# A third Strassen product of the second block's MLP output map made from seven quarter products

## The chip, the cores and the metric

The kernel runs on one core of one Trainium2 chip. The metric is the device time of one execution in microseconds (us); less is better. TensorE (PE in the profile) multiplies, VectorE (DVE) and ScalarE (ACT) work element by element, GpSimd (POOL) and SyncE (SP) mostly issue transfers.

## The reference

One decoder layer on 2048 tokens of width 1024: a token-mixing sub-layer (an input projection, a gated short convolution, a causal pooling, an output projection) and an MLP of hidden width 4096, each closed by a residual sum and a LayerNorm.

```
h = x * (1.0 + sc1) + sh1
z = h @ w_in[l]
...
x = _layer_norm(DEEPNORM_ALPHA * x + (1.0 + g1) * mix, ln1_g[l], ln1_b[l])
h = x * (1.0 + sc2) + sh2
f = jnp.square(jax.nn.relu(h @ w_mlp_in[l])) @ w_mlp_out[l]
x = _layer_norm(DEEPNORM_ALPHA * x + (1.0 + g2) * f, ln2_g[l], ln2_b[l])
```

The change sits in the second matrix of the MLP, `w_mlp_out` (4096 by 1024).

## The kernel before

**Blocks.** The tokens are worked in two blocks of 1024 (b = 0 and 1), one after the other: input projection (in_proj_1 for block 1), output projection with the first LayerNorm, `up()` (the first MLP map with the squared ReLU) and `down()` (the second map, with the second LayerNorm in the class Close).

**Precision.** Each fp32 operand is split into a high part (a ScalarE cast, L81) and a low part (a VectorE subtraction, L82), and a product is three matmuls, high by high, high by low, low by high (L86 to L88, in `mm3`). The low part waits for the cast, and the matmuls wait for both. `tt` (L91) is the helper for all other VectorE sums.

**Seven products for eight.** The large products are cut into 2 by 2 blocks and made by Strassen's scheme in Winograd's form, seven products instead of eight:

```
ORDER = (("11", "11"), ("12", "21"), ("s2", "2"), ("s1", "1"), ("s3", "3"), ("s4", "22"), ("22", "4"))
```

Each entry names the left block or sum (U, the activations; s1 to s4 are sums of blocks) and the right one (W; 1 to 4 are sums). `up()` makes the U blocks and their sums and stores them in DRAM (`usum`, or `uquart` for those needed in quarters); `down()` loads them with the weights, splits them and multiplies.

**down() of block 1.** Products are taken in steps: a coarse product i has two halves (hf) of four operand pairs, and each half is 96 matmuls of 128x512 into four PSUM banks X[0..3] or Y[0..3], one for each of four tiles of 128 tokens. In most steps the loop is over operands, then tiles; in the second halves of products 3, 4 and 6 ("by tile") it is over tiles, then operands, so that each tile's result can be finished while the next is made. Products 1 and 5 are "fine": each is again made as seven products of quarter blocks, each of 48 matmuls of 128x256 (L1118), with sums in SBUF tiles F[0..7]. Before, the order is product 0 (two steps), the 14 fine products, then 2, 3, 4 and 6. The finished rows are handled by `third_row` and `first_row` (tiles 0 to 3, behind product 3), `second_row` (behind 4) and `last` and `last_part` (tiles 4 to 7, behind 6, the tail of the kernel; tile 7 is cut into two column quarters). They add the banks, multiply by the gate (`gate`, g2), add the saved residual (`rsave`) and normalise.

**residual()** loads the normalised input `nsave[t]` of each token tile, scales and shifts it by two VectorE operations, and stores it in `rsave[t]`; `down()` lets it go on by two tiles a step from step n = 2.

**Sums for quarters.** A fine product needs sums of quarter blocks: of U, made by `save_quarters` in `up()`, and of W, made by `sum_blocks` behind `up()`'s later groups g (QUARTER_SUMS says how many behind each) and stored in `wquart`.

**Order.** The queue of each engine is fixed when the program is built: the framework schedules the instructions in a list, and each engine works strictly along its own. So an instruction that waits holds up everything behind it on its engine. Buffers rotate through pools (t_r, t_w, t_h, t_o and t_ps for PSUM banks).

## Time and profile before

| | us |
|---|---|
| Median of three runs | 1734.39 (1733.82 to 1734.42) |
| Profiled execution, its own time | 1734.73 |
| Its span in the trace | 1733.0 |
| TensorE busy in the span | 1720.9 (99%) |
| VectorE busy | 1342.6 (77%) |
| ScalarE busy | 879.5 (51%) |

The times are those of one execution of the whole program; the span runs from its first to its last instruction. A row of a timeline reads: start, duration, engine, line, operation, tile written and tiles read with shapes, and in brackets the idle time ahead of it with what ended it. Matmuls are pipelined, so their durations overlap, and the distance between starts is what one costs; the same holds, by some 0.08 us, for VectorE. In a list of waits a row gives the total, how many and the longest. The granted clock was 0.999 of full speed.

### The profile page before, as it was taken

To read this page: it belongs to the slowest core of one execution; us is meant where nothing else is said; L and a number is where in the kernel's file an instruction comes from. 1 tells how busy PE (TensorE), PEld (TensorE's weight loads), DVE (VectorE), ACT (ScalarE), POOL (GpSimd) and SP (SyncE) were. 2 spreads that over 40 slices of the span, in tenths; PEclk is the share of its full clock that TensorE was granted. 3 is DMA by queue.
4 is the path that set the end of the run, shared out by engine and by line. 5 is a ranking of instruction groups with operands and counts; after the bars stand their busy time and mean duration, and the time that the engine had idled before them with its cause. 6 is when DMAs were issued, how large, how long until landed. Compare 5 with 4: busy or idle time off the path is not lost.

```text
span 1733.0 us, 22349 instructions
## 1 busy us (share of the span) xinstructions
PE 1720.9 (99%) x7998; PEld 1439.4 (83%) x7998; DVE 1342.6 (77%) x1759; ACT 879.5 (51%) x1188; POOL 235.7 (14%) x441
## 2 busy tenths in 40 slices
PE   9999999999999999999999999999999999999997
PEld 8888888888888888888888888888888888998886
DVE  8898798877777676769686779687677768987894
ACT  5323358554454654436573344775444565763451
POOL 0222221122322000000000000103222221000000
PEclk9999999999999999999999999999999999999999
DMA  9899867778888998887572265657655599998871
GB/s 385 343 322 357 321 229 282 280 272 318 327 320 325 366 413 326 303 289 270 190 273 79 104 236 201 218 196 263 248 205 213 201 325 409 417 362 311 285 257 49
DMA packets 149646, 480.47 MB, mean 277 GB/s; under 512 B 17680, under 2 KB 18464, under 8 KB 149536
## 3 DMA queue, kind: packets, MB, share of 16 engines
q1 hardware_dynamic: 102528, 313.87, 49.8%
q0 software_dynamic: 47008, 165.19, 25.0%
q8 instruction: 62, 1.02, 0.2%
q14 instruction: 48, 0.39, 0.1%
HBM read 329.56 MB, written 149.43 MB: 276 GB/s over the span
## 4 chain that ended last, share of the span: by engine, by line
PE 95%; DVE 2%; issue 2%; DMA 1%; ACT 0%; POOL 0%; SPq 0%; DVEq 0%; POOLq 0%; ACTq 0%
PE ps L86 29%; PE ps L87 29%; PE ps L88 29%; PE ps L1118 5%; PE ps L406 3%; PE ps L757 1%; DVE o L91 1%; DMA r<-msum 1%; DMA msum<-o 0%; DMA r<-in_opening 0%; DVE o L1333 0%; DVE o L1339 0%; DVE o L261 0%; DVE st L726 0%; DVE h L82 0%
## 5 line engine op out<-in xcount | busy, mean ns | idle before, releaser
L87 PE MATMUL ps<-h,w 128*128 128x512 f32 x1312 | 510.3, 389 | 0.0
L88 PE MATMUL ps<-h,w 128*128 128x512 f32 x1312 | 510.1, 389 | 0.0
L86 PE MATMUL ps<-h,w 128*128 128x512 f32 x1312 | 510.1, 389 | 0.0
L86 PE MATMUL ps<-h,h 128*128 128x512 f32 (+1 forms) x1000 | 387.9, 388 | 2.2 <-DVE o L91 1.7
L88 PE MATMUL ps<-h,h 128*128 128x512 f32 (+1 forms) x1000 | 387.7, 388 | 0.0
L87 PE MATMUL ps<-h,h 128*128 128x512 f32 (+1 forms) x1000 | 387.5, 387 | 0.0
L81 ACT CAST h<-r 128x1024 fp32r<-128x1024 f32 (+1 forms) x196 | 199.4, 1021 | 279.0 <-PE ps L87 147.5
L82 DVE TENSOR_TENSOR h<-r,h 128x1024 fp32r<-128x1024 f32 (+1 forms) x196 | 230.9, 1182 | 83.4 <-ACT h L81 83.1
L81 ACT CAST w<-r 128x1024 fp32r<-128x1024 f32 x156 | 164.2, 1053 | 257.0 <-PE ps L87 251.2
L87 PEld LDWEIGHTS ps<-h,w 128*128 128x128 f32 x1312 | 246.3, 188 | 51.8 <-DVE h L82 0.5
L88 PEld LDWEIGHTS ps<-h,w 128*128 128x128 f32 x1312 | 246.3, 188 | 51.1
L86 PEld LDWEIGHTS ps<-h,w 128*128 128x128 f32 x1312 | 246.0, 188 | 51.4 <-issue 0.3
L82 DVE TENSOR_TENSOR w<-r,w 128x1024 fp32r<-128x1024 f32 x156 | 190.6, 1222 | 96.5 <-ACT w L81 95.5
L86 PEld LDWEIGHTS ps<-h,h 128*128 128x128 f32 x1000 | 187.8, 188 | 41.3 <-DVE o L91 1.9
L88 PEld LDWEIGHTS ps<-h,h 128*128 128x128 f32 x1000 | 187.8, 188 | 38.5
L87 PEld LDWEIGHTS ps<-h,h 128*128 128x128 f32 x1000 | 187.8, 188 | 38.0
L91 DVE TENSOR_TENSOR o<-o,o 128x1024 f32<-128x1024 f32 (+2 forms) x218 | 186.0, 859 | 42.8 <-DMA usum<-o 39.2
L82 DVE TENSOR_TENSOR h<-w,h 128x1024 fp32r<-128x1024 f32 x124 | 151.2, 1219 | 4.9 <-ACT h L81 4.8
L91 DVE TENSOR_TENSOR o<-o,ps 128x512 f32<-128x512 f32 (+1 forms) x172 | 112.4, 664 | 48.6 <-PE ps L88 48.2
L81 ACT CAST h<-w 128x1024 fp32r<-128x1024 f32 x124 | 130.0, 1049 | 9.5 <-DMA w<-in_w 4.3
L1003 POOL DMA_DIRECT2D usum<-o x96 | 51.7, 538 | 431.9 <-ACT o L997 195.8
L91 DVE TENSOR_TENSOR r<-r,r 128x1024 f32<-128x1024 f32 x60 | 73.4, 1223 | 11.4 <-DMA r<-in_w 7.6
(151 smaller groups left out, 1419.3 us busy)
## 6 DMA issues: line engine op xcount, KB each, us to landing
usum<-o POOLq DMA_DIRECT2D x96, 512.0 KB, 4.2
r<-usum SPq DMA_DIRECT2D x96, 512.0 KB, 5.3
w<-w2sum SPq DMA_DIRECT2D x64, 512.0 KB, 6.1
r<-in_w SPq DMA_DIRECT2D x60, 512.0 KB, 5.8
o<-in_w SPq DMA_DIRECT2D x72, 256.0 KB, 5.8
w2sum<-o POOLq DMA_DIRECT2D x64, 256.0 KB, 6.0
w<-in_w SPq DMA_DIRECT2D x32, 512.0 KB, 6.0
r<-uquart SPq DMA_DIRECT2D x28, 512.0 KB, 9.5
```

The lines of the kernel that those rows point to most:

```text
L81: high = nc.scalar.copy(hi, src)
L82: return high.ins, nc.vector.tensor_tensor(lo, src, hi.bitcast(F32), op=ALU.subtract).ins
L86: nc.tensor.matmul(ps, whi, xhi, start=first, stop=False, skip_group_check=goes_on)
L87: nc.tensor.matmul(ps, whi, xlo, start=False, stop=False, skip_group_check=goes_on)
L88: nc.tensor.matmul(ps, wlo, xhi, start=False, stop=last, skip_group_check=goes_on)
L91: return nc.vector.tensor_tensor(out_, a, b_, op=op)
L406: nc.tensor.matmul(ps[m, h], wt[:, w : w + P], A[k][p // 2][:, hs], start=k == 0 and p == 0, stop=k == KD - 1 and p == 2)
L757: nc.tensor.transpose(ps[:, t * P : t * P + P], R[4 * h + t][:, k * P : k * P + P], ident)
L1003: nc.gpsimd.dma_start(usum[g, i], r)
L1118: nc.tensor.matmul(ps, a[:, us], w[:, gs], start=not begun, stop=hf == 1 and g == 3 and a is ul, skip_group_check=True)
```

## The change

Product 0 of block 1's map (11 by 11) becomes fine too: `FINE` gets an entry for it, and `coarse` drops it, so 192 matmuls of 128x512 give way to 336 of 128x256. The order is now product 2 (coarse), 21 fine products (0, 1, 5), then 3, 4, 6.

- The quarters of product 0 are summed in F[4..7]. ScalarE copies them once to the other half; after product 1 and after product 5 four VectorE adds join them to F[0..3], and after product 5 product 2's banks X are added as well. `third_row` now adds (it copied), and `last` adds the bank to F before the gate, where the gate read the bank.
- The sums of W quarters and some of U quarters are generators in two `Spare` lists. `sums_beside.step()` puts the next VectorE operation of such a sum behind a product: 14 steps in groups 1 and 2 of `in_proj_1`, the rest in `up()` from g = 1. The weights for it come as whole 128x1024 tiles (`w2s`). For g = 0 and 1 the block of U for product 0 is stored whole and loaded again for its quarter sums.
- `residual()` begins at step 0 and gives its eight tiles in five turns, ending at 0, 1, 4, 6 and 7.
- For tile 7 the first halves are added ahead of the last step, and its last two quarters go to two PSUM banks of their own (`ps = t_ps()`), where both used X[3].
- In `in_proj_1`'s last group `pool_mid` stands behind the first half of the convolution.

The core of the diff (line numbers of helpers move by one, L82 becomes L81, L91 becomes L90):

```diff
+    class Spare:
+        def __init__(self):
+            self.items = []
+            self.current = None
+
+        def add(self, item):
+            self.items.append(item)
+
+        def step(self, n=1):
+            for _ in range(n):
+                while True:
+                    if self.current is None:
+                        if not self.items:
+                            return
+                        self.current = self.items.pop(0)
+                    if next(self.current, self) is not self:
+                        break
+                    self.current = None
...
+    sums_beside, quarters_beside = Spare(), Spare()
+
+    def quarter_sums(n, hf, p):
+        a, b_ = t_o(T), t_o(T)
+        b22, b12, b11, b21 = a[:, :H], a[:, H:], b_[:, :H], b_[:, H:]
+        for i, r in enumerate((a, b_)):
+            nc.sync.dma_start(r, w2s[n, hf, p, i])
+        yield
+        tt(b22, b22, b12, ALU.subtract)
+        yield
+        tt(b12, b12, b11, ALU.subtract)
+        yield
+        tt(b11, b22, b11, ALU.add)
+        yield
+        tt(b21, b21, b11, ALU.subtract)
+        for i, r in ((2, b22), (0, b12), (1, b11), (3, b21)):
+            nc.gpsimd.dma_start(wquart[n, hf, i][:, p * H : p * H + H], r)
+
+    for n_ in (2, 0, 1):
+        for hf_ in range(2):
+            for p_ in range(2):
+                sums_beside.add(quarter_sums(n_, hf_, p_))
...
+        def beside_(j):
+            if 0 < j < NG - 1:
+                sums_beside.step()
...
-                pt = pool_mid(1, j, v)
...
+                    pt = pool_mid(1, j, v)
...
-    FINE = {1: 0, 5: 1}
+    FINE = {0: 2, 1: 0, 5: 1}
+    QUARTERED = {1: 0, 7: 1, 0: 2}
...
-            if fine and i in (1, 7):
-                save_quarters(r, i // 4, g)
-            else:
-                nc.gpsimd.dma_start(usum[g, i], r)
+            if fine and i in QUARTERED and (i or g > 1):
+                item = save_quarters(r, QUARTERED[i], g)
+                quarters_beside.add(item)
+                if i == 0:
+                    kept.append(item)
+                return
+            nc.gpsimd.dma_start(usum[g, i], r)
+            if fine and i == 0:
+                sums_beside.items.insert(0, save_quarters(None, QUARTERED[i], g, True))
...
+        def beside_():
+            if fine and g:
+                quarters_beside.step(2)
+                if g > 1:
+                    sums_beside.step()
...
-            if t % 2:
+            if t in ends:
...
-        coarse = (0, 2, 3, 4, 6) if b else (0, 1, 2, 3, 5, 4, 6)
+        coarse = (2, 3, 4, 6) if b else (0, 1, 2, 3, 5, 4, 6)
...
-            return [F[2 * row + t][:, c : c + Q] for t in range(2)]
+            return [F[(0 if i else 4) + 2 * row + t][:, c : c + Q] for t in range(2)]
...
+                ps = t_ps()
                 for n, (uh, ul, wh, wl) in enumerate(ops):
                     for p in range(2):
                         cs = slice(p * H + 3 * P, p * H + 4 * P)
                         ws_ = slice(p * H + c, p * H + c + Q)
-                        mm3(banks[3][:, c : c + Q], uh[:, cs], ul[:, cs], wh[:, ws_], wl[:, ws_],
-                            False, n == len(ops) - 1 and p == 1, True)
-                last_part(slice(c, c + Q), banks[3][:, c : c + Q])
+                        mm3(ps[:, :Q], uh[:, cs], ul[:, cs], wh[:, ws_], wl[:, ws_],
+                            n == p == 0, n == len(ops) - 1 and p == 1)
+                last_part(slice(c, c + Q), ps[:, :Q])
...
-            keep(t + 4, hi_, ps)
+            add(t + 4, hi_, ps)
...
+            if b:
+                tt(F[t + 4][:, lo_], F[t + 4][:, lo_], ps, ALU.add)
+                ps = F[t + 4][:, lo_]
...
-            table[0] = X, True, lambda t, ps: None
-            table[2] = X, False, lambda t, ps: add(t, hi_, ps)
+            table[2] = X, True, lambda t, ps: None
             table[3] = Y, True, third_row
-        base = 2 if b else 5
+        base, turns = (0, 5) if b else (5, 4)
...
-        later = residual()
+        later = residual((0, 1, 4, 6, 7) if b else (1, 3, 5, 7))
...
+                if b and i == 6:
+                    add(7, lo_, X[3])
+                    gate(7, lo_)
+                    tt(rest[6][3], rest[6][3], F[7][:, lo_], ALU.add)
...
-                    if m == 6:
-                        for t in range(4):
-                            add(t, lo_, X[t])
+                    if part_ < 6:
+                        continue
+                    for t in range(4):
+                        if k == 0:
+                            nc.scalar.copy(F[t + 4][:, hi_], F[t + 4][:, lo_])
+                            continue
+                        cs = lo_ if k == 1 else hi_
+                        tt(F[t][:, cs], F[t][:, cs], F[t + 4][:, lo_], ALU.add)
+                        if k == 5:
+                            add(t, hi_, X[t])
...
-        else:
-            sums = [(sum_blocks, [w2q[n, i, hf] for i in range(4)], wquart[n, hf], p)
-                    for n in range(2) for hf in range(2) for p in halves]
```

The change shows in the queues at these three places, the first two on VectorE and TensorE, the third on VectorE.

VectorE in `in_proj_1` of block 1, where group 3's product 2 begins. `w` low parts come from L82 (now L81); the `ps` rows add product 1's two banks, L261 and L265 (now L260 and L264) are steps of the pooling and the convolution. Before:

```order
L326 SCALAR_TENSOR_TENSOR o_7867<-o_7792,vecs,o_7867 128x1024
L643 COPY o_8046<-uhalo 128x2
L82 TENSOR_TENSOR w_8150<-r_8047,w_8149 128x1024
L327 SCALAR_TENSOR_TENSOR o_7867<-o_7792,vecs,o_7867 128x1024
L91 TENSOR_TENSOR o_7867<-o_7867,o_7868 128x1024
L261 TENSOR_TENSOR o_8121<-o_7791 128x1039
L82 TENSOR_TENSOR w_8180<-r_8144,w_8179 128x1024
L91 TENSOR_TENSOR o_8045<-o_8045,ps_8093 128x512
L261 TENSOR_TENSOR o_8123<-o_8121 128x1037
L91 TENSOR_TENSOR o_8046<-o_8046,ps_8106 128x512
```

Now:

```order
L326 SCALAR_TENSOR_TENSOR o_7895<-o_7810,vecs,o_7895 128x1024
L90 TENSOR_TENSOR r_8089<-r_8089,r_8088 128x1024
L260 TENSOR_TENSOR o_8162<-o_7809 128x1039
L90 TENSOR_TENSOR o_7895<-o_7895,o_7896 128x1024
L260 TENSOR_TENSOR o_8164<-o_8162 128x1037
L90 TENSOR_TENSOR o_8086<-o_8086,ps_8134 128x512
L260 TENSOR_TENSOR o_8166<-o_8164 128x1033
L90 TENSOR_TENSOR o_8087<-o_8087,ps_8147 128x512
L264 SCALAR_TENSOR_TENSOR o_8168<-o_8166,o_7809 128x1024
L81 TENSOR_TENSOR w_8191<-r_8088,w_8190 128x1024
```

The split that gives product 2's first low weights (w_8150 before, w_8191 now) stood ahead of both bank adds and stands behind them and behind the L264 step.

TensorE at the same place. The bank ps_8100 is product 2's first; w_8190 is the high and w_8191 the low part of its weights. Now:

```order
L87 MATMUL ps_8147<-h_7065,w_8131 128x512
L85 MATMUL ps_8100<-h_7074,w_8190 128x512
L86 MATMUL ps_8100<-h_7075,w_8190 128x512
L85 MATMUL ps_8113<-h_7074,w_8190 128x512
L86 MATMUL ps_8113<-h_7075,w_8190 128x512
L85 MATMUL ps_8224<-h_7288,w_8220 128x512
L87 MATMUL ps_8100<-h_7074,w_8191 128x512
L85 MATMUL ps_8100<-h_7074,w_8190 128x512
L86 MATMUL ps_8100<-h_7075,w_8190 128x512
```

Five matmuls come between product 1's last and the first that reads w_8191; before, the third matmul of the product read w_8150.

VectorE in `down()` of block 1, from `third_row`'s first tile (bank ps_13212 before, ps_13542 now). Before:

```order
L91 TENSOR_TENSOR o_11442<-o_11442,ps_13212 128x512
L91 TENSOR_TENSOR o_11442<-o_11442,bc_4830 128x1024
L1323 SCALAR_TENSOR_TENSOR o_11442,mv_13399<-o_11442,r_13396 128x512 x2
L734 TENSOR_SCALAR mv_13399<-mv_13399 128x1
L1333 SCALAR_TENSOR_TENSOR o_13406<-o_11442,mv_13399,w_13402 128x1024
```

Now:

```order
L90 TENSOR_TENSOR o_11540<-o_11540,ps_13542 128x512
L90 TENSOR_TENSOR o_11536<-o_11536,ps_13542 128x512
L90 TENSOR_TENSOR o_11536<-o_11536,bc_4830 128x1024
L90 TENSOR_TENSOR r_13690<-r_13690,o_11640 128x1024
L90 TENSOR_TENSOR r_13695<-r_13695,o_11640 128x1024
L90 TENSOR_TENSOR r_13690<-r_13690,o_11642 128x1024
L90 TENSOR_TENSOR r_13695<-r_13695,o_11642 128x1024
L1429 SCALAR_TENSOR_TENSOR o_11536,mv_13729<-o_11536,r_13726 128x512 x2
L90 TENSOR_TENSOR o_11541<-o_11541,ps_13543 128x512
```

One more add and four operations of the residual (r_13690 and r_13695 are tiles 5 and 6) have come between; the residual's were ahead of `third_row` before.

VectorE at the end of that list, the last splits for product 4's second half. Before:

```order
L719 TENSOR_SCALAR mv_13545<-mv_13545 128x1
L82 TENSOR_TENSOR h_13597<-w_13590,h_13596 128x1024
L718 RECIPROCAL mv_13545<-mv_13545 128x1
L82 TENSOR_TENSOR h_13605<-r_13600,h_13604 128x1024
L82 TENSOR_TENSOR h_13609<-w_13602,h_13608 128x1024
```

Now:

```order
L81 TENSOR_TENSOR h_13915<-w_13908,h_13914 128x1024
L775 RECIPROCAL mv_13875<-mv_13875 128x1
L81 TENSOR_TENSOR h_13923<-r_13918,h_13922 128x1024
L81 TENSOR_TENSOR h_13927<-w_13920,h_13926 128x1024
L81 TENSOR_TENSOR h_13935<-r_13930,h_13934 128x1024
L90 TENSOR_TENSOR r_13942<-r_13942,o_11640 128x1024
L81 TENSOR_TENSOR h_13939<-w_13932,h_13938 128x1024
```

An operation of the residual's tile 7 (r_13942) stands ahead of the last split.

TensorE there; h_13934 and h_13938 are the last operand pair's high parts, h_13935 and h_13939 its low ones, ps_11651 and ps_11652 the banks of the first and second tile. Now:

```order
L87 MATMUL ps_11651<-h_13926,h_13923 128x512
L85 MATMUL ps_11651<-h_13938,h_13934 128x512
L85 MATMUL ps_11652<-h_13902,h_13898 128x512
L86 MATMUL ps_11652<-h_13903,h_13898 128x512
L87 MATMUL ps_11652<-h_13902,h_13899 128x512
L85 MATMUL ps_11652<-h_13902,h_13898 128x512
L86 MATMUL ps_11651<-h_13939,h_13934 128x512
L87 MATMUL ps_11651<-h_13938,h_13935 128x512
```

Four matmuls of the second tile stand ahead of the first that reads h_13939; before, the tile's matmuls stood in one row without them.

VectorE in the tail, tile 4 of eight and the start of tile 5 (L783 is L726 before, L1439 is L1333, L1445 is L1339). Before:

```order
L91 TENSOR_TENSOR o_11446<-ps_11546,bc_4830 128x512
L91 TENSOR_TENSOR o_11446<-o_11446,r_14020 128x512
L726 BN_STATS st_13789<-o_11446 128x6
L730 BN_AGGR mv_14052<-st_13789 128x2
L719 TENSOR_SCALAR mv_14052<-mv_14052 128x1
L718 RECIPROCAL mv_14052<-mv_14052 128x1
L1333 SCALAR_TENSOR_TENSOR o_14050<-o_11446,mv_14052,w_13402 128x1024
L1339 SCALAR_TENSOR_TENSOR o_14050<-o_14050,mv_14052,w_13404 128x1024
L91 TENSOR_TENSOR o_11447<-ps_11547,bc_4830 128x512
```

Now:

```order
L90 TENSOR_TENSOR o_11540<-o_11540,ps_11651 128x512
L90 TENSOR_TENSOR o_11540<-o_11540,bc_4830 128x512
L90 TENSOR_TENSOR o_11540<-o_11540,r_14355 128x512
L783 BN_STATS st_14124<-o_11540 128x6
L787 BN_AGGR mv_14391<-st_14124 128x2
L776 TENSOR_SCALAR mv_14391<-mv_14391 128x1
L775 RECIPROCAL mv_14391<-mv_14391 128x1
L1439 SCALAR_TENSOR_TENSOR o_14389<-o_11540,mv_14391,w_13732 128x1024
L1445 SCALAR_TENSOR_TENSOR o_14389<-o_14389,mv_14391,w_13734 128x1024
L90 TENSOR_TENSOR o_11541<-o_11541,ps_11652 128x512
```

Each tile has one more L90 row, the add of the bank.

More of the change, by code (lines that the diff above doesn't have):

```diff
@@ L44, in tile_hybrid_layer @@
 def tile_hybrid_layer(ctx: ExitStack, tc: tile.TileContext, opening, xT, x, wada, vec, win0, win,
-                      wins, wpool, wout, wmix, w1, w2, w2q, rows, out):
+                      wins, wpool, wout, wmix, w1, w2, w2q, w2s, rows, out):
     nc = tc.nc
@@ L1009, in up @@
         save(c11, 0)
+        beside_()
         yield
@@ L1033, in up @@
             join(c12, Z)
+            beside_()
+        for item in kept:
+            quarters_beside.finish(item)
         s1 = t_o()
@@ L1047, in up @@
         save(c11, 7)
+        beside_()
+        if fine and g == NC - 1:
+            quarters_beside.step(99)
+            sums_beside.step(99)
     def down_operands(i, gs):
@@ L1064, in down_operands, with residual @@
         return out_, done
-    def residual():
+    def residual(ends):
         ag, ab = row(t_o(D), rows[0]), row(t_o(D), rows[1])
@@ L1146, in down, with matmuls @@
         fine_banks = {}
-        def matmuls(banks, ops, new, begins, ends, then, by_tile, cut=False):
+        def matmuls(banks, ops, new, begins, ends, then, by_tile, cut=False, closes=False):
             if new and begins:
@@ L1162, in matmuls @@
                     mm3(banks[t], uh[:, cs], ul[:, cs], wh[:, ws_], wl[:, ws_],
-                        new and begins and n == p == 0, ends and n == len(ops) - 1 and p == 1, not new)
+                        new and begins and n == p == 0,
+                        (ends or closes and t == 3) and n == len(ops) - 1 and p == 1, not new)
                 if ends and n == len(ops) - 1:
@@ L1394, in mlp @@
                 pass
-            some = (QUARTER_SUMS if b else HALF_SUMS)[g]
+            some = HALF_SUMS[g]
             for make, src, dst, p in sums[:some]:
```

45 lines of the change are left out of this document (36 added, 9 removed).

## The prediction

> **What bounds it now.** I read the page first, then its chain of work, then TensorE's list of waits.
>
> ```profile
> PE 1720.9 (99%) x7998; PEld 1439.4 (83%) x7998; DVE 1342.6 (77%) x1759; ACT 879.5 (51%) x1188; POOL 235.7 (14%) x441
> PE 95%; DVE 2%; issue 2%; DMA 1%; ACT 0%; POOL 0%; SPq 0%; DVEq 0%; POOLq 0%; ACTq 0%
> PE ps L86 <- DVE o L91: 1.7, 1, 1.7
> PE ps L120 <- DVE tmp L115: 1.1, 1, 1.1
> PE ps L406 <- ACT h L222: 0.6, 1, 0.6
> PE ps L86 <- ACT o L628: 0.6, 1, 0.6
> ```
>
> TensorE is busy for 99% of the span and is 95% of the chain; in the whole run it waits four times, 4.0 us together. So the time moves in only two ways: TensorE gets less or more to stream, or a wait comes or goes. The waits must be looked for where VectorE or ScalarE prepares operands with little time to spare, because VectorE gets most of the added work. An average of 77% says nothing about those places.
>
> **The product itself.** Chain and timeline give the first matmul of the coarse product 0, the first fine one, and the whole fine stage; then ScalarE's two longest waits in that stage (total, times, longest), and a window of it (columns: PE, PEld, DVE, ACT, POOL busy, clock, DMA share, GB/s).
>
> ```profile
> 1424.18 0.39 PE L86 MATMUL ps<-h,h 128*128 128x512 f32 x1
> 1467.70 0.76 PE L1118 MATMUL ps<-h,h 128*128 128x256 f32 x5
> 1467.87 80.63 PE ps L1118 x672
> 1548.50 0.23 PE ps L86
> ACT h L81 <- PE ps L1118: 15.6, 22, 0.9
> ACT h L81 <- DMA r<-uquart: 0.6, 3, 0.3
> 1468.00:1488.00 20.00, 20.00 (x169) 20.00 (x169) 18.45 (x18) 16.23 (x20) 0.00 (x0) 1.00 1.03 418
> ```
>
> The coarse product takes 1467.70 − 1424.18 = 43.52 us for 192 matmuls, 0.2267 each. The fine stage takes 80.63 us for 672, 0.1200 each. Seven quarter products are 7 × 48 = 336 matmuls, 40.32 us. Term 1 is 40.32 − 43.52 = **−3.2 us**. This holds as long as TensorE stays the bound of the longer fine stage. ScalarE waits there for TensorE to free operand buffers, not the other way, VectorE has 1.55 us of 20 free, and the adds between the groups (four of 0.6) fall into operands prepared a product ahead. The DMA share of 1.03 is full, with the transfers still ahead of the casts; I cost it at nothing and keep it as a rival.
>
> [...] The rows (226.7 and 120.0) show a fixed part of 2 × 120.0 − 226.7 = 13.3 ns for these fp32r triples, so halving the columns pays less, and I keep −3.2.
>
> **The sums moved into the mixing projection (in_proj_1).** Fourteen steps of the quarter sums now stand behind products of its groups 1 and 2. Going through the order, I find one place where a split that TensorE is about to need moves behind them: the switch to group 3's product 2.
>
> ```profile
> 992.00:1014.00 22.00, 22.00 (x98) 18.20 (x97) 21.93 (x23) 10.06 (x14) 0.71 (x1) 1.00 0.32 112
> 1000.36 1.22 DVE L82 TENSOR_TENSOR w<-r,w 128x1024 fp32r<-128x1024 f32 x1
> 1006.24 0.68 DVE L91 TENSOR_TENSOR o<-o,ps 128x512 f32<-128x512 f32 x1
> 1006.84 1.23 DVE L261 TENSOR_TENSOR o<-o 128x1037 f32<-128x1037 f32 x1
> 1007.99 0.68 DVE L91 TENSOR_TENSOR o<-o,ps 128x512 f32<-128x512 f32 x1
> 1010.87 1.22 DVE L265 SCALAR_TENSOR_TENSOR o<-o,o 128x1024 f32<-128x1024 f32 x1
> 1007.44 0.39 PE L88 MATMUL ps<-h,w 128*128 128x512 f32 x1
> 1007.67 0.39 PE L86 MATMUL ps<-h,w 128*128 128x512 f32 x1
> ```
>
> VectorE works 21.93 of 22 us here. The split that gives this product's low weights ran at 1000.36, 7.3 us ahead of its first matmul at 1007.67. In the changed order it stands behind the add of product 1's second bank, which cannot begin before that bank is done (the row at 1007.99), and behind the last step of the convolution. So 1007.99 + 0.60 (add; rows 1006.24 and 1006.84 stand 0.60 apart) + 1.2 (L265) + 1.14 (split) = 1010.9. The matmul order fills in five others first, so the low part is needed at 1007.67 + 5 × 0.2267 = 1008.8. Term 2 is **+2.1 us**. Bounds: 0, if scheduling makes an operand look later than it is, and 4, if the extra work ahead (two weight sums and the wait-free adds) makes the queue another 2 us late. I take 2.1, as these rows give it directly.
>
> The later end of this projection had one wait:
>
> ```profile
> 1044.62 0.48 ACT o L628
> 1045.14 0.50 PE ps L86
> ```
>
> The last mixed sums are placed three to four VectorE operations earlier relative to their neighbours, and TensorE arrives 2 us later, so the copy at L628 should no longer be late: term 3, **−0.6 us** (0 if it stays).
>
> **The sums moved into up().** Two VectorE operations behind each product, some 12 us in all.
>
> ```profile
> 1130.00:1423.00 293.00, 293.00 (x1295) 242.32 (x1294) 215.84 (x257) 154.89 (x182) 61.64 (x103) 1.00 0.63 231
> ```
>
> VectorE has 77 us idle in 293, and the DMA share is 0.63. The cover is that idle time; without it the 12 us would stand on the path at most once. The closing quarter sums of before disappear here, and residual tiles take their place. The transfers count too: an item loads two 512 KB tiles on SyncE's queue and stores four slices on GpSimd's (22 and 24 more instructions there in the whole order), at a DMA share of 0.63. The four copies that ScalarE makes once after the first seven products are of 0.5 us each (its L628 copy, above), in a stage where it works 16.23 of 20. I cost all this at **0** (−1 to +2).
>
> **The end of the map: product 4, second half.** This is the place to watch. Coarse steps are 21.76 us. The rows give the starts of product 3's second half (1613.64) and product 4's second half (1657.16), and VectorE between them.
>
> ```profile
> 1616.00:1638.00 22.00, 22.00 (x99) 18.22 (x98) 21.17 (x32) 8.61 (x18) 1.07 (x2) 1.00 0.76 266
> 1638.00:1661.00 23.00, 23.00 (x103) 19.04 (x102) 23.00 (x37) 19.19 (x34) 0.00 (x0) 1.00 0.88 299
> 1612.76 1.23 DVE L91 TENSOR_TENSOR r<-r,o 128x1024 f32<-128x1024 f32 x1 [6.58 <-DMA r<-nsave]
> 1616.18 3.62 DVE L91 TENSOR_TENSOR r<-r,o 128x1024 f32<-128x1024 f32 x3
> 1621.98 0.68 DVE L91 TENSOR_TENSOR o<-o,ps 128x512 f32<-128x512 f32 x1
> 1655.73 1.21 DVE L82 TENSOR_TENSOR h<-w,h 128x1024 fp32r<-128x1024 f32 x1
> 1656.87 1.21 DVE L82 TENSOR_TENSOR h<-r,h 128x1024 fp32r<-128x1024 f32 x1
> 1613.64 0.39 PE L86 MATMUL ps<-h,h 128*128 128x512 f32 x1
> 1657.16 0.39 PE L86 MATMUL ps<-h,h 128*128 128x512 f32 x1
> ```
>
> From the first add of third_row (1621.98) to the end of the last split that product 4's second half needs (1656.87) VectorE is solidly busy: 34.9 us. This step goes tile by tile, so all four operands are needed within its first tile. The same list in the changed order holds four more bank adds (0.60 each, 2.4) and five more residual operations (3.53 / 3 = 1.18 to 1.14 each, 5.7): 34.9 + 8.1 = 43.0 us. When may it begin? Not before the first tile of product 3 is done, 5.6 us after that step's start, and in before it began 8.3 after it (1621.98 − 1613.64), held up by residual loads (the 6.58). So it ends 48.6 to 51.3 after the start. The new matmul order fills in four matmuls of the second tile, so the last low part is needed 43.52 + 23 × 0.2267 = 48.7 after it. The wait is 0 to 2.6, and more if one of the queue's own waits (a residual load, a square root on ScalarE) grows: up to 5. Term 4 is **+2 us**, near the row 1621.98, because the same loads and more splits stand ahead of the list.
>
> **The tail.** Tiles 4 to 6 of the last product get one more bank add each; the last two quarters go to banks of their own.
>
> ```profile
> 1706.32 0.69 DVE L91 TENSOR_TENSOR o<-ps,bc 128x512 f32<-128x512 f32 x1 [15.97 <-PE ps L88]
> 1707.05 0.69 DVE L91 TENSOR_TENSOR o<-o,r 128x512 f32<-128x512 f32 x1
> 1711.76 0.69 DVE L91 TENSOR_TENSOR o<-ps,bc 128x512 f32<-128x512 f32 x1
> 1721.22 0.42 DVE L91 TENSOR_TENSOR o<-ps,bc 128x256 f32<-128x256 f32 x1
> 1721.69 0.39 PE L86 MATMUL ps<-h,h 128*128 128x256 f32 x1 [1.66 <-DVE o L91]
> 1724.87 0.42 DVE L91 TENSOR_TENSOR o<-ps,bc 128x256 f32<-128x256 f32 x1 [1.24 <-PE ps L88]
> 1726.24 0.26 DVE L730 BATCH_NORM_AGGREGATE mv<-st 128x2 f32<-128x24 f32 x1
> ```
>
> VectorE needs 5.44 us a tile (1711.76 − 1706.32), the same as 24 matmuls, so it only just keeps up. One more add of 0.73 (1707.05 − 1706.32) in each of three tiles makes VectorE the bound: the tiles start at 1706.32, 1712.49 and 1718.66. The 1.66 us that TensorE waited for VectorE's read of the shared bank disappear, and the second quarter's sums would be ready by 1724.87 − 1.66 = 1723.2; but VectorE, 2.2 us late, aggregates the last tile's statistics at 1727.2 instead of 1726.24. Term 5 is **+0.95 us** (0.5 to 1.5), and the vanished wait is worth nothing.
>
> **Sum.** −3.2 + 2.1 − 0.6 + 0 + 2.0 + 0.95 = +1.25 against the profiled run's own 1734.73 (span 1733.0): 1736.0. The median of the runs shown is 1734.39, 0.34 lower, so 1735.6. A measurement here can tell about 0.2%, 3.5 us, from no change.
>
> **Rivals.** (a) Both new waits are absorbed, because the splits are ready: −3.2 − 0.6 + 0.95 = −2.85, 1731.5. For it: the margins are 2 us out of long queues. Against it: VectorE shows no idle time in either place. (b) The other side: the list before product 4's second half begins 8.3 us or later and one of its ten small waits on ScalarE, or a residual load behind the full DMA queues (share 0.88), costs 2 to 3 us more. It decides from a wait of 4.5 us there. With 5 us, and the other terms as summed, +4.3: 1738.7; with 4 at term 2 as well, 1740.6. (c) The longer fine stage is bound by its transfers: a share of 1.03 over 121 us instead of 81. For it: ScalarE waits for `uquart` three times, 0.6 us in all; against it: TensorE never did in 80 us. If 40 us of it ran 5% late, +2: 1737.6. (d) The product's gain is kept whole, with the terms at their low ends (0, −0.6, −1, 0, +0.5): −4.3, 1730.1, faster.
>
> **Numbers.** The forecast gets 0.40 (1733.5 to 1737.8), (a) 0.24, (b) 0.20, (c) 0.06, (d) 0.10. Slower by over 0.2% (above 1737.9) takes (b), half of (c) and the forecast's upper edge: 0.29. Faster (below 1730.9) takes (d) and a little of (a): 0.13. The rest, 0.58, is within. For 8 times in 10 the range reaches from 1731.0 into (a) to 1741.0, the end of (b).
>
> **What would show it.** Fine stage: 1008 matmuls in 121 us without a wait. In the list of TensorE's waits, one on a weight's split (L81) of about 2 us near 1009 and one on an operand's split near the middle of the last coarse steps; neither the wait for L628's successor nor the 1.7 on the shared bank. VectorE's tail tiles 6.17 us apart. I'm wrong if the splits are ready in time at both places, or if TensorE waits in the fine stage or in up().

## The result, and the profile after

The changed kernel takes 1747.41 us (median of 4 runs, 1743.96 to 1748.01) against 1734.2 for the one before: ratio 1.0072, 95% interval 1.0055 to 1.0090. It is slower by about 13 us, outside the forecast's range. The profiled execution took 1748.01 us with a span of 1746.2.

Busy times, chain of work and TensorE's waits of the changed kernel:

```profile
PE 1722.0 (99%) x8142; PEld 1444.0 (83%) x8142; DVE 1382.4 (79%) x1839; ACT 891.0 (51%) x1208; POOL 256.7 (15%) x475
PE 76%; issue 13%; DMA 5%; DVE 3%; POOL 1%; ACT 1%; SPq 0%; DVEq 0%; POOLq 0%; ACTq 0%
PE ps L86 <- DVE h L81: 4.6, 5, 1.5
PE ps L1209 <- ACT o L1219: 2.6, 1, 2.6
PE ps L87 <- DVE w L81: 2.2, 2, 2.0
PE ps L85 <- DVE o L90: 1.9, 3, 0.8
PE ps L119 <- DVE tmp L114: 1.1, 1, 1.1
PE ps L85 <- ACT o L1053: 1.0, 1, 1.0
PE ps L405 <- ACT h L221: 0.6, 1, 0.6
```

TensorE is still at 99%, but the chain is TensorE for 76% and not 95%: from 1302 us on, in `up()` and behind it, it runs through loads, GpSimd's stores and VectorE. The waits are 14.0 us where they were 4.0. None is large, and they lie in five places.

To place them, I sum for each stage how much later each matmul starts than the one before it plus 0.2267 us (128x512) or 0.1200 (128x256). "Lost" below is that sum; some 0.3 of the first column is in every run. The last column runs from the last matmul's start to the end.

| lost, us | in_proj_1, out_proj | up() | start of down() | fine stage | products 3, 4, 6 | tail |
|---|---|---|---|---|---|---|
| before | 1.2 | 0.2 | 0 | 0 | 1.9 | 8.4 |
| changed | 2.6 | 4.9 | 1.1 | 2.9 | 4.9 | 10.4 |

The difference of the spans, 13.2 us, is made of: in_proj_1 +1.4, `up()` +4.7, start of down() +1.1, the product −3.2, fine stage +2.9, the last products +3.0, tail +1.9, and +1.1 from the first 10 us, where the clock was granted 2.4 us later in this execution (matmuls of 128x128 start 0.213 us apart at first and 0.111 apart from 7.64 us on, before from 5.24; both programs are the same there). These add up to 12.9.

### The profile page after: what moved, and what is told of

Same layout as the page of the kernel before. It is cut to its first block, busy times and chain, and to the rows that moved or that the text cites. A ratio compares the mean times of both kernels' runs of the same rounds, so it can differ in the third digit from the quotient of the medians.

```text
span 1746.2 us, 22853 instructions
## 1 busy us (share of the span) xinstructions
PE 1722.0 (99%) x8142; PEld 1444.0 (83%) x8142; DVE 1382.4 (79%) x1839; ACT 891.0 (51%) x1208; POOL 256.7 (15%) x475
## 4 chain that ended last, share of the span: by engine, by line
PE 76%; issue 13%; DMA 5%; DVE 3%; POOL 1%; ACT 1%; SPq 0%; DVEq 0%; POOLq 0%; ACTq 0%
PE ps L87 24%; PE ps L86 24%; PE ps L85 24%; PE ps L405 3%; DVE o L90 1%; DMA o<-in_w2s 1%; DMA usum<-o 1%; PE ps L814 1%; DMA uquart<-o 1%; DVE h L81 1%; DMA rsave<-r 0%; DVE o L1445 0%; DMA r<-in_opening 0%; DVE o L1439 0%; DMA r<-usum 0%
## 5 line engine op out<-in xcount | busy, mean ns | idle before, releaser
L86 PE MATMUL ps<-h,h 128*128 128x512 f32 (+1 forms) x936 | 363.1, 388 | 4.6 <-DVE h L81 4.6
L85 PE MATMUL ps<-h,h 128*128 128x512 f32 (+1 forms) x936 | 362.8, 388 | 0.1
L87 PE MATMUL ps<-h,h 128*128 128x512 f32 (+1 forms) x936 | 362.8, 388 | 0.0
L80 ACT CAST h<-r 128x1024 fp32r<-128x1024 f32 (+1 forms) x202 | 205.6, 1021 | 252.8 <-PE ps L86 109.0
L81 DVE TENSOR_TENSOR h<-r,h 128x1024 fp32r<-128x1024 f32 (+1 forms) x202 | 237.9, 1182 | 71.5 <-ACT h L80 71.2
L81 DVE TENSOR_TENSOR w<-r,w 128x1024 fp32r<-128x1024 f32 x156 | 190.4, 1220 | 78.8 <-ACT w L80 78.2
L90 DVE TENSOR_TENSOR o<-o,o 128x1024 f32<-128x1024 f32 (+2 forms) x250 | 202.9, 819 | 45.1 <-DMA usum<-o 38.4
L86 PEld LDWEIGHTS ps<-h,h 128*128 128x128 f32 x936 | 175.8, 188 | 42.3 <-DVE h L81 6.6
L85 PEld LDWEIGHTS ps<-h,h 128*128 128x128 f32 x936 | 175.8, 188 | 36.5 <-ACT h L80 0.5
L87 PEld LDWEIGHTS ps<-h,h 128*128 128x128 f32 x936 | 175.8, 188 | 35.4
L81 DVE TENSOR_TENSOR h<-w,h 128x1024 fp32r<-128x1024 f32 x130 | 158.2, 1217 | 7.5 <-ACT h L80 7.5
L90 DVE TENSOR_TENSOR o<-o,ps 128x512 f32<-128x512 f32 (+1 forms) x182 | 117.5, 654 | 45.9 <-PE ps L87 41.1
L80 ACT CAST h<-w 128x1024 fp32r<-128x1024 f32 x130 | 136.5, 1050 | 6.5 <-DMA w<-w2sum 2.1
L1209 PE MATMUL ps<-h,h 128*128 128x256 f32 x1008 | 121.4, 283 | 2.6 <-ACT o L1219 2.6
L1209 PEld LDWEIGHTS ps<-h,h 128*128 128x128 f32 x1008 | 121.1, 192 | 2.9 <-ACT o L1219 2.8
```

The lines of the kernel that those rows point to most:

```text
L80: high = nc.scalar.copy(hi, src)
L81: return high.ins, nc.vector.tensor_tensor(lo, src, hi.bitcast(F32), op=ALU.subtract).ins
L85: nc.tensor.matmul(ps, whi, xhi, start=first, stop=False, skip_group_check=goes_on)
L86: nc.tensor.matmul(ps, whi, xlo, start=False, stop=False, skip_group_check=goes_on)
L87: nc.tensor.matmul(ps, wlo, xhi, start=False, stop=last, skip_group_check=goes_on)
L90: return nc.vector.tensor_tensor(out_, a, b_, op=op)
```

## The experiments

The edits are against the changed kernel unless said otherwise. "Late residual" is e3.

### Where the residual stands

```diff
-        base, turns = (0, 5) if b else (5, 4)
+        base, turns = (0, 2) if b else (5, 4)      # e2, ends (3, 7)
+        base, turns = (2, 4) if b else (5, 4)      # e3, ends (1, 3, 5, 7)
```

Early: 

> The changed kernel with all eight residual tiles in the two steps of product 2 (four in each). Theory (five residual operations in VectorE's list make the splits of product 4's second half late; residual tiles ahead of the fine stage hold the buffers its loads need): the 3.8 us of waits in product 4 fall to under 1, the wait early in the fine stage grows from 2.6 to 4 or more; the time changes by under 2 us. Rival (the four bank adds and VectorE's late start make the splits late): product 4 keeps 3 us or more of waits, and the time is 1 to 3 us above the changed kernel.

Late: 

> The changed kernel with residual() from step 2 on, two tiles in each of four steps, all behind the fine stage. Theory: no residual tile holds a buffer ahead of the fine stage, so its early wait of 2.6 us and the loss of 1 us at the start of down() vanish, while VectorE's list before product 4's second half gets 3.4 us longer and the waits there grow from 3.8 to 6 to 8; the time stays within 2 us of the changed kernel. Rival (the fine stage starts short of operands because up() ends late): the 2.6 us stay, and the time is 2 to 4 us above.

Early took 1757.04 us (ratio 1.0131, 1.0116 to 1.0146), late 1741.23 (1.0038, 1.0025 to 1.0051). With the residual early product 4 loses nothing, and the fine stage 19.7 us; its waits there:

```profile
PE ps L1209 <- DVE h L81: 6.9, 3, 4.9
PE ps L1209 <- ACT h L80: 3.1, 2, 2.7
PE ps L1209 <- ACT o L1219: 2.0, 1, 2.0
```

With it late the fine stage loses nothing, as expected, and product 4 nothing either, which I had expected to lose 6 to 8: the scheduler put the four residual operations of step 4 behind the last splits. What stays is 1.5 us at product 6, where TensorE waits for banks. The loss at the start of down() stayed at 1.1, so the residual does not cause that. In `up()` e2, e3 and e5 (below) have the changed kernel's order on every engine, and yet their profiles lose 1.2, 1.8 and 3.0 us there, where it lost 4.9. So the 4.9 is the figure of one execution. In the late residual's profile the clock dropped behind the wait near 1012 (0.66 of full speed from 1011 to 1016 us) and TensorE lost some 1.6 us there, ahead of `up()` (last section); whether that has to do with it was not tested. The residual's place is a cause of the loss in product 4, and ahead of the fine stage it is one of two conditions of the loss there (the other is below).

### Where the sums stand

```diff
# e4: in_proj_1's beside_ does nothing
-            if 0 < j < NG - 1:
-                sums_beside.step()
+            pass
# e1: that, U's sums at once, and in mlp(), behind each group of up()
+                for _ in range((0, 3, 2, 2, 2, 2, 2, 1)[g]):
+                    for _ in sums_beside.items.pop(0):
+                        pass
```

> The changed kernel without sums behind the products of in_proj_1; all stand one operation behind each product of up(), and what is left over behind its last group. Theory: the wait of 2.0 us near 1012 vanishes; the three and a half items are made at the end of up(), where they add to the lost time there: 1745 to 1750 us, with 5 us or more lost in up() and at the start of down(). Rival (the split is late near 1012 for another cause): the wait there stays at 2 us.

> The changed kernel, but no sums stand in in_proj_1, the quarter sums of U are made at once as before, and the quarter sums of W as whole items behind each group of up() (3, 2, 2, 2, 2, 2, 1 items behind groups 1 to 7). Theory 1 (the sums spread one operation behind each product cost the time: their loads come late and VectorE, in order, holds the bank adds): the wait of 2.0 us near 1012 and the 4.8 us lost in up() between 1380 and 1430 vanish, some 6 to 7 us less than the changed kernel, about 1740 us. Rival (the added transfers of the third product's sums cost it, wherever they stand): up() still loses 3 to 5 us and only the 2 us at 1012 go, about 1745. The 2.6 us early in the fine stage should stay if residual() causes it, and go if up()'s late end does; the 3.8 us in product 4 stay in both.

Without sums in in_proj_1 the wait near 1012 is gone in both, so they cause it. The time grows, to 1752.49 (e4; 1.0104, 1.0087 to 1.0121) and 1755.65 (e1; 1.0120, 1.0103 to 1.0137): e4 loses 10.3 us from the start of down() to the first fine matmul, and 6.3 in the fine stage; e1 loses 17.6 in `up()` and 8.3 in the fine stage. Theory 1 put e1 at 1740. With all sums in `up()`, whole items (e1) are no faster than spread ones (e4), so it is not the spreading that costs.

### What of the sums costs it

Traffic, or what the sums hold: in e7 and e10 the last eight W items become transfers from DRAM to DRAM of the same bytes.

```diff
+            with tc.issue_after(stored[-1].ins):     # e10 only; stored: GpSimd's last usum store
+                nc.gpsimd.dma_start(wquart[n, hf, i][:, p * H : p * H + H],
+                                    w2s[n, hf, p, i // 2][:, i % 2 * H : i % 2 * H + H])
```

> The changed kernel with the last eight W quarter items left out as sums: their slots are filled by transfers from DRAM to DRAM of unsummed quarters, one behind each product, so the same bytes land in the same place but no SBUF buffer is held and VectorE has no operation. The output is not the layer's. Theory (VectorE waits in order for the items' loads and buffers in up()): the 4.8 us lost in up() at 1380 to 1430 and the 1.1 us at the start of down() vanish, the 2.0 us at 1012, the fine stage's 2.9 and product 4's 4.8 stay: 1741 to 1743 us. Rival (the traffic itself costs it): up() loses 3 us or more as before.

> The changed kernel with the last eight W quarter items replaced by transfers from DRAM to DRAM, one behind each product of up() at the places of the items' steps (held there behind GpSimd's stores), so that the bytes move beside up() but no SBUF buffer is held and VectorE has no operation for them. The output is not the layer's. Theory (buffers and VectorE's waits, not traffic, cost the time): up() loses under 1 us, the fine stage too. Rival (the traffic and GpSimd's queue cost it): up() loses 3 us or more.

In e7 nothing held the copies back: all 32 went out in the first 40 us and cost the kernel's start some 18 us (1757.23, ratio 1.0135, 1.0114 to 1.0156), so it says nothing on traffic beside `up()`; without the items, `up()`, the start of down() and the fine stage lose no more than before the change. In e10 they stand there, and `up()` loses 0.2 us, the start of down() and the fine stage nothing, with the residual where the change has it: 1739.07 (1.0029, 1.0018 to 1.0040), 8.3 us under the changed kernel. TensorE has no wait from 1130 to 1440. VectorE's longest there:

```profile
DVE w L81 <- ACT w L80: 38.4, 21, 4.1
DVE o L90 <- DMA usum<-o: 20.6, 7, 3.7
DVE o L90 <- PE ps L87: 15.3, 13, 2.1
```

VectorE waits 15.3 us for TensorE here; in the changed kernel, in the same window, for the sums' loads:

```profile
DVE o L90 <- DMA o<-in_w2s: 23.6, 9, 5.8
DVE o L90 <- DMA usum<-o: 21.2, 7, 4.7
```

The kernel before made 24 operations of such sums in this stage (1130 to 1423 us there), and none of its waits is for their loads:

```profile
DVE w L82 <- ACT w L81: 32.7, 18, 4.2
DVE o L91 <- DMA usum<-o: 22.1, 7, 4.2
DVE o L91 <- PE ps L88: 13.8, 11, 2.1
```

So the bytes are not the cost; the items' loads, SBUF buffers and VectorE operations are, for 4.7 us in `up()` and 4.0 behind it. One of these waits in rows (SyncE's queue, then VectorE):

```profile
1317.28 16.30 SPq L501 DMA_DIRECT2D r<-in_w  x4
1333.69 0.86 SPq L648 DMA_DIRECT2D o<-in_w2s  x2
1340.75 0.69 DVE L90 TENSOR_TENSOR o<-o 128x512 f32<-128x512 f32 x1 [4.33 <-DMA o<-in_w2s]
```

The load goes out behind four weight loads and lands 7 us later; VectorE stands 4.33 us, with the bank adds behind. At the end of `up()` such a wait reaches TensorE and ScalarE:

```profile
1423.36 0.69 DVE L90 TENSOR_TENSOR o<-o 128x512 f32<-128x512 f32 x1 [5.85 <-DMA o<-in_w2s]
1424.71 0.50 PE L85 MATMUL ps<-h,w 128*128 128x512 f32 x1 [0.83 <-DVE o L90]
1428.44 1.06 ACT L1062 ACTIVATE o<-o 128x1024 f32<-128x1024 f32 x1 [12.45 <-DVE o L90]
```

Three runs look for what makes the load late; the ring is the pool of 12 buffers of `t_o`.

```diff
# e9, the last eight items: three yields between the loads and the first tt, then two tt per step
# e13
-            nc.sync.dma_start(r, w2s[n, hf, p, i])
+            nc.scalar.dma_start(r, w2s[n, hf, p, i])
# e18
-        return mk(big, [P, w], dt, "o", 12)
+        return mk(big, [P, w], dt, "o", 11)
```

> The changed kernel, in which each W quarter item of up() (the last eight) is loaded three products ahead of its first operation, not one; its four operations then stand two behind each of two products, and it holds its two buffers as long as before. Theory A (VectorE waits in order for loads issued one product, 5.4 us, ahead, while a load takes 7 us or more): VectorE's 21.6 us of waits for the w2s loads fall below 5 and up()'s loss from 4.9 us to under 2; about 1742 us. Theory B (the buffers that the items hold make the other allocations wait): up() still loses 4 us or more, with VectorE or ScalarE waiting for usum stores; no better than the changed kernel.

> The changed kernel with one edit: the loads of the W quarter items are issued on ScalarE's queue, not SyncE's. Theory (in SyncE's in-order queue these loads stand behind the weight loads of up(), which wait for buffers): VectorE's 23.6 us of waits for them in up() fall below 8, up()'s loss from 4.9 to under 2 us, and with it the 1.1 at the start of down() and the fine stage's 2.9 get smaller: 1740 to 1743 us. Rival (the items' SBUF buffers are the last to come free): VectorE's waits stay at 15 us or more and up() still loses 3 us or more; ScalarE, held by its own loads, may even add some.

> The changed kernel with 11 buffers in that ring, not 12, and nothing else. If buffers are what up() is short of, VectorE's waits for w2s loads and usum stores there (44.8 us together) grow by 8 us or more and up() loses 8 us or more, not 4.9; the fine stage's early wait grows with it. Rival (buffers are not short; the operations' places in VectorE's order are): up()'s loss stays within 1.5 us of 4.9.

e9: 1746.85 (1.0073, 1.0058 to 1.0088); VectorE's waits for the loads are 18.8 us and `up()` loses 2.7. But the edit hardly reached the queues: the loads keep their places on SyncE, and the first operation of six of the eight items keeps its place on VectorE, the other two stand one and two places later. So e9 says nothing on an earlier load; e3, with the changed kernel's order in `up()`, has 17.8 and 1.8.

e13: 1755.06 (1.0113, 1.0099 to 1.0127); the waits are 27.1 us and `up()` loses 10.7. On ScalarE's queue the load goes out just as VectorE comes to it, behind work of ScalarE that had itself waited for VectorE:

```profile
1291.67 1.06 ACT L1062 ACTIVATE o<-o 128x1024 f32<-128x1024 f32 x1 [4.35 <-DVE o L90]
1292.93 0.85 ACTq L648 DMA_DIRECT2D o<-in_w2s  x2
1298.82 0.69 DVE L90 TENSOR_TENSOR o<-o 128x512 f32<-128x512 f32 x1 [6.04 <-DMA o<-in_w2s]
```

So e13 only puts the loads behind another queue that is held up, and does not clear SyncE's. In the changed kernel SyncE's own waits between 1130 and 1440 us are, for the weight loads (L501) and the sums' loads (L648):

```profile
SPq L501 <- DVE o L90: 156.3, 14, 24.2
SPq L648 <- DMA wquart<-o: 0.2, 1, 0.2
```

The sums' loads wait 0.2 us for buffers of their own. They go out late because loads ahead of them in the queue wait for VectorE (six times of eight a weight load, as in the kernel before, where these wait 132.5 us), and they land 6.3 to 10.7 us after they go out. No run lets them pass those loads, so what that would give back stays open.

e18: 1749.39 (1.0086, 1.0071 to 1.0101); the waits are 24.1 and 21.7, `up()` loses 5.5; one buffer fewer hardly matters there, as the rival said, though the fine stage's early wait grew from 2.6 to 3.6 us.

```diff
# e17: items in two buffers of their own, the ring shrunk to 10
+        a, b_ = t_q(), t_q()
```

> The changed kernel in which the W quarter items have two buffers of their own, taken from the ring of 12 that the U blocks, their sums and the items share (ring 10 and 2). Theory (in one ring the two buffers that an item holds for four products make other tiles wait for them, and the item's loads wait for the U blocks' stores): VectorE's waits for the w2s loads in up() fall from 23.6 to under 12 us and those for usum stores stay near 21; up() loses under 3 us, not 4.9. Rival (it is simply too few buffers in all): the waits for usum stores grow by 5 us or more and up() loses as much as before or more.

e17 did not test the ring: with buffers that nothing else uses, the scheduler put the items into block 0, all 24 loads in the first 500 us, and block 0 lost some 80 us (1820.45; 1.0497, 1.0479 to 1.0514). But it makes all sums, early, and from 930 to 1700 us TensorE has no wait at all: not near 1012, not in `up()`, not in the fine stage with the residual ahead of it. Product 4's waits stay (4.1 us). That agrees with e10. What the traces show is that the items' loads come late for VectorE; whether an earlier load or a later place in VectorE's order would mend it stays open.

### The parts together

```diff
# e5: late residual, and ahead of the last step, for tiles 4 to 6
+                        gate(t + 4, lo_)
+                        tt(rest[6][t], rest[6][t], F[t + 4][:, lo_], ALU.add)
# and in last()
-                tt(F[t + 4][:, lo_], F[t + 4][:, lo_], ps, ALU.add)
# e6: late residual, no step behind products 4 to 6 of in_proj_1's group 2, up() from g = 1
# e8: e5 and e6; e11: e8 with up() from g = 2; e12: e11 with e9's loads; e14: e11 with e13's loads
# e15: e14 with turns (2, 3), ends (2, 5, 7); e16: e15 with e9's loads
```

> The kernel with the late residual, and beside that the tail as before in length: for tiles 4 to 6 the sum in F is gated and added to the saved residual ahead of the last step, so that last() has two VectorE operations between the bank and the statistics and not three. Theory (VectorE bounds the tail at 6.17 us a tile): the tiles stand 5.44 us apart again, and the time is 1 to 2 us below the late residual's, 1739 to 1740 us. Rival (another wait bounds the end): the same as the late residual within 0.5 us.

The tail is 8.9 us after the last matmul, where the late residual has 10.4, and the tiles stand 5.44 apart. So the extra add is worth 1.5 us at the end. The whole did not get measurably faster (1740.34; 1.0033, 1.0022 to 1.0043): in its profile `up()` lost 3.0 and not 1.8, and TensorE lost 2.6 us at product 6 and not 1.5, where the operations now stand.

> The kernel with the late residual, and no sum behind products 4 to 6 of in_proj_1's group 2 (11 steps there, not 14); up() takes the steps from its group 1 on, not 2. Theory: the split near 1010 is in time, so the 2.0 us of wait and the half-speed stretch behind it (1.6 us) vanish; up() begins its sums earlier and ends them earlier, so its waits at 1422 to 1431 do not grow: 3 us or more below the late residual's, 1737 to 1738 us. Rival (each sum costs wherever it stands): up() loses what in_proj_1 gains, no change.

> Late residual, tail sums ahead and fewer in_proj steps together. Theory: the parts add up, 1735 to 1737 us, about the kernel before. Below 1731 would need up() free of waits too. Rival: 1739 or more, because up() takes back what in_proj_1 gains.

e6: 1749.0 (1.0084, 1.0070 to 1.0098), e8: 1745.28 (1.0069, 1.0056 to 1.0081). The wait near 1012 goes, and `up()` loses 16.7 and 13.9, of it 8.6 and 8.7 in one wait near 1155, in the group where the steps now begin. The rival held.

> Late residual, tail sums ahead, no sums behind products 4 to 6 of in_proj_1's group 2, and up() starting its sums from group 2 as in the changed kernel; three more steps are left for the end of up(). Theory: the 8.7 us wait near 1155 of the kernel with all three parts came from up()'s group 1 steps and vanishes, in_proj_1 loses nothing, up() 2 to 3 us, the start of down() 1 to 3 more: 1735 to 1738 us. Rival: up()'s end loses what in_proj_1 gains, 1740 or more.

> As the kernel with fewer steps and late up(), and the items of up() loaded three products ahead. Theory A: up() loses under 1.5 us: 1733 to 1736 us. Theory B: the same as without, 1736 to 1740.

e11: 1741.31 (1.0038, 1.0023 to 1.0053); in_proj_1 loses nothing, `up()` 5.2, product 6's banks 3.3. e12: 1739.87 (1.0029, 1.0018 to 1.0039), `up()` 1.7. Its queues differ from e11's as little as e9's do from the changed kernel's, so the lead is not what it shows. It is level with the late residual, and none of these beats the kernel before.

> The kernel with fewer steps and late up() (late residual, tail sums ahead, 11 steps in in_proj_1) with the W quarter loads on ScalarE's queue. Theory: up() under 2 us, about 1736 to 1738 us; rival: no better than without, 1739 or more.

> As the one before, with residual() in three turns (tiles 0 to 2, 3 to 5, 6 and 7 at steps 2, 3 and 4), all ahead of product 4's second half. Theory (the wait on X's banks at product 6 comes from residual tiles 6 and 7 standing ahead of second_row): that wait (2 to 3 us) vanishes and none comes back in product 4: 1733 to 1736 us. Rival: the residual tiles of step 4 make product 4's splits late again, 3 us or more there.

> As the one before, and the items of up() loaded three products ahead. If both the queue and the lead matter, up() loses under 1 us and the kernel stands at 1731 to 1734 us, level with the kernel before or up to 0.2% better; the product itself gives 3.2 us. Rival: 1736 or more, because the items still hold buffers that VectorE waits for.

e14: 1745.13 us (1.0062, 1.0048 to 1.0076), e15: 1749.07 (1.0082, 1.0069 to 1.0094), e16: 1748.19 (1.0073, 1.0059 to 1.0086). All three lose 12.8 to 15.3 us in `up()`; e13, with the loads on the same queue, lost 10.7. Products 4 and 6 lose 2.2 together in e15 and 5.5 in e16, where the residual stands in the same turns, so what three turns do there is not settled.

## Why the prediction was wrong, step by step

**The product, −3.2: right.** The fine stage's first matmul is at 1476.25, the next stage begins at 1600.1; less the 2.9 lost that is 121.0 us for 1008 matmuls, 0.1200 each.

**in_proj_1, +2.1: right, by its own rows.** VectorE:

```profile
1009.00 0.69 DVE L90 TENSOR_TENSOR o<-o,ps 128x512 f32<-128x512 f32 x1 [0.17 <-PE ps L87]
1009.61 1.22 DVE L264 SCALAR_TENSOR_TENSOR o<-o,o 128x1024 f32<-128x1024 f32 x1
1010.75 1.22 DVE L81 TENSOR_TENSOR w<-r,w 128x1024 fp32r<-128x1024 f32 x1
1012.02 0.50 PE L87 MATMUL ps<-h,w 128*128 128x512 f32 x1 [1.99 <-DVE w L81]
```

The split stands where it was put, and TensorE waits 1.99 us. The wait at L628's copy is gone, **−0.6: right**.

**The sums in up(), 0 (−1 to +2): wrong, and this is the step that failed.** It cost 4.7 us there and 4.0 behind it in the profile (e10 takes all of it away, and its median is 8.3 us lower). The prediction compared 12 us of operations with 77 us of idle time, and a DMA share of 0.63, as if an operation only took its own time. The 12 us were right: VectorE is busy for 226.8 us of this stage (1130 to 1431.4 us), where it was for 215.8 (1130 to 1423). (The count of transfers was not: 6 more on SyncE's queue and 34 more on GpSimd's in the traces, not 22 and 24.) But VectorE works in order, and these operations wait: 23.6 us for nine loads, which stand on SyncE's queue behind other loads that wait. What stood behind them, bank adds and splits, was late with them, and so were the U blocks' stores and the first operands of down(). That is a wait behind which a queue stands, which the prediction asked about for in_proj_1 and for product 4, and not for this stage. No rival held it either.

**The fine stage, covered: half right.** Its steady run has no wait, and transfers did not bound it (rival (c) did not come). But it begins short of operands:

```profile
1488.89 1.04 ACT L80 CAST h<-r 128x1024 fp32r<-128x1024 f32 x1 [1.13 <-DMA r<-uquart]
1489.84 0.64 ACT L1219 COPY o<-ps 128x256 f32<-128x256 f32 x2
1490.54 0.63 PE L1209 MATMUL ps<-h,h 128*128 128x256 f32 x3 [2.61 <-ACT o L1219]
```

ScalarE's copy of a bank stands behind casts that wait for `uquart` loads, and the third product needs that bank. Either a late residual (e3, e5) or an `up()` that ends in time (e10) removes it: it takes both the early residual and the late end. The residual tiles moved ahead of this stage were the part of the change that I followed only to product 4.

**Product 4, +2.0 (0 to 2.6, up to 5): mechanism right, size off.** VectorE's list begins 7.0 us after product 3's second half (1628.86 less 1621.86; 5.6 to 8.3 were given) and ends at 1675.35, 46.5 us long and not 43.0. In it, with ScalarE, SyncE and GpSimd:

```profile
1628.86 1.28 DVE L90 TENSOR_TENSOR o<-o,ps 128x512 f32<-128x512 f32 x2
1636.24 0.53 POOL L1168 DMA_DIRECT2D rsave<-r  x1 [0.60 <-DVE r L90]
1644.24 0.79 SPq L1146 DMA_DIRECT2D r<-usum  x2
1650.17 1.05 ACT L80 CAST h<-r 128x1024 fp32r<-128x1024 f32 x1 [5.88 <-DMA r<-usum]
1652.82 0.21 DVE L797 TENSOR_SCALAR mv<-mv 128x1 f32<-128x1 f32 x1 [5.12 <-ACT tmp L793]
1674.21 1.22 DVE L81 TENSOR_TENSOR h<-w,h 128x1024 fp32r<-128x1024 f32 x1
1667.29 0.50 PE L86 MATMUL ps<-h,h 128*128 128x512 f32 x1 [1.52 <-DVE h L81]
```

A residual tile is stored (1636.24), its buffer comes free, the operand load goes out (1644.24), the cast waits 5.88 us for it (1650.17), L793 stands behind the cast on ScalarE, and VectorE waits 5.12 us for L793. The prediction named such a wait as the way to 5 us and left it out of the sum. The matmuls fill in around it, so TensorE loses 3.8 us in four waits and some 0.9 beside them (behind a wait the second matmul starts 0.34 us after the first, 1667.29 and 1667.63, where others start 0.23 apart).

**The tail, +0.95: too much.** First add of tile 4, tile 5, the last quarter's add, the last aggregation:

```profile
1719.56 0.69 DVE L90 TENSOR_TENSOR o<-o,ps 128x512 f32<-128x512 f32 x1 [3.30 <-PE ps L87]
1725.69 0.68 DVE L90 TENSOR_TENSOR o<-o,ps 128x512 f32<-128x512 f32 x1
1736.94 0.42 DVE L90 TENSOR_TENSOR o<-ps,bc 128x256 f32<-128x256 f32 x1
1739.38 0.27 DVE L787 BATCH_NORM_AGGREGATE mv<-st 128x2 f32<-128x24 f32 x1
```

The tiles stand 6.13 apart, as foreseen, but from the first add to the aggregation it is 19.8 us, and 19.9 before. The quarters' operations now stand between others and cost less than in a row of their own (below). The vanished wait and the longer tiles cancel out: 0.

**The rest.** The late clock at the start, +1.1 in this execution, has nothing to do with the change. With what was measured the sum is −3.2 + 1.4 + 8.7 (`up()` and what follows from it) + 4.9 (product 4) + 0 (tail) + 1.1 (clock) = +12.9.

## What to carry to other kernels

An operation put into an idle engine's in-order queue costs what it waits, not what it works (here VectorE waited 23.6 us for nine loads and worked 11.0 us more): price its load, what stands ahead of that load in its queue, and everything that stands behind the operation, and count on idle time only where its inputs are already there. When a stage that prepares operands gets later, look at the stage behind it too: its loads, buffers and casts begin late together (here 2.6 us at the third fine product). A gain of 3 us on the bounding engine needs every added operation to be free, and here each place that took them gave the time back.

## What the runs showed of the hardware

**A 2.0 us wait was followed by a loss of 1.6 us more in one profile, and not in another.** The wait near 1012 is 1.99 us in the changed kernel and in the late residual. In the changed kernel the matmuls behind it start 0.23 us apart (1013.07, 1013.31, 1013.53). In the late residual the clock is granted at half for a while, and eight matmuls take 3.38 us (1012.56 to 1015.94), 0.42 each, where 8 × 0.2267 is 1.81. The changed kernel, then the late residual, windows with the clock in the third column from the end:

```profile
1011.00:1016.00 5.00, 3.98 (x17) 3.29 (x18) 5.00 (x7) 0.59 (x1) 2.00 (x3) 1.00 0.78 238
1011.00:1016.00 5.00, 4.48 (x13) 3.56 (x14) 5.00 (x7) 0.67 (x2) 2.13 (x4) 0.66 0.76 256
```

The wait is as long in both, so its length alone does not decide; what does is not shown. Nor is it shown whether this is part of why the changed kernel's times lie 4 us apart; its fastest and its slowest run have the same mean clock, 0.998.

**In the tail, VectorE operations that need each other's result stand further apart.** Four rows of 128x512 that use the one before stand 0.73 us apart (1719.56 to 1721.74 in the changed tail), independent ones 0.60 (1006.24 and 1006.84 before). In the last full tile the quarters' operations stand between such rows, and the distances are 0.61, 0.33 and 0.60 us (1733.25, 1733.86, 1734.19, 1734.79): from its first add to the aggregation it is 7.57 us, where the forecast had 8.5. That is what the tail's forecast had too high.
